# Moving the low half of the key rows from GpSimd to VectorE in the expert stage

## The chip, the cores and the metric

The kernel runs on one core of one Trainium2 chip. The metric is the device time of one execution in microseconds, the median of several. TensorE (PE), VectorE (DVE), ScalarE (ACT), GpSimd (POOL) and SyncE (SP) each work through an instruction list of their own in a fixed order and wait for each other by semaphores. Plain transfers are issued from SP's queue, gathers from POOL's queue; 16 DMA engines carry both.

## The reference

Two transformer blocks over 512 tokens of width 1024. Each ends with a mixture of 16,384 single-row experts, which is what the change touches. Cut to that part (the first block's; the second block's is the same function with other names):

```
q = (xb @ w_q).reshape(PEER_BLOCK, PEER_HEADS, 2, PEER_QDIM // 2)
s = jnp.einsum('thsd,hsnd->thsn', q, sub_keys).astype(jnp.float32)
sv, si = lax.top_k(s, PEER_TOPK)
...
e = jnp.take_along_axis(cidx, pos, axis=-1)
g = jax.nn.softmax(top, axis=-1)
act = jax.nn.gelu(jnp.einsum('thkd,td->thk', u_tab[e], xb), approximate=False)
w = (g * act).astype(xb.dtype)
return jnp.einsum('thk,thkd->td', w, v_tab[e])
```

Every token picks 8 x 16 = 128 experts. Each picked expert has a key row in `u_tab` and a value row in `v_tab`, both 1024 wide. The result is the sum of the value rows, weighted by gate times gelu(key row . token).

## The kernel before

The function `peer` (line 1071) runs once per block, so twice in the program. Its long stage is the loop over `e` in `range(128)` (line 1255): one step is one block of 128 experts. The 512 tokens are treated in two ways.

The first three tiles of 128 tokens (384 tokens) are done densely. `emit_A` makes the products of a block's 128 key rows with all 384 tokens: `a_dma` loads the block's transposed key rows `ur` (line 1094), `a_hi` rounds them to a high half `uh` on ACT (line 1099), `a_lo` makes the low half `ul = ur - uh` (line 1105), and `a_mm` multiplies: 24 matmuls (lines 1112, 1113, 1115), then a gelu into `ga`. Products run 28 blocks ahead (`NA = 28`), so that step `e` makes block `e + 28`, up to step 99. Then step `e` multiplies `ga` by the gates of block `e` (`gbuf`, loaded once for four blocks) to `w`, splits `w` into `wh` (ACT, line 1268) and `wl` (DVE, line 1269) and the value rows `vr` into `vh` (ACT) and `vl` (DVE, line 1263), and adds 18 matmuls into `y` (lines 1293 to 1295).

The last tile of 128 tokens is done by gathers. For each of 128 slots, `g_u` has POOL gather one key row per token into `urow` (line 1229), and DVE multiplies it with the tokens and sums (line 1230). `g_v` gathers the value rows into `vrow` (line 1241), and DVE adds them, weighted, into `acc` (line 1243). That makes 256 gathers in a stage, 128 rows of 4 KB each, into three buffers of `urow` and three of `vrow`. The first 32 or so are `urow` alone, then both kinds alternate, and the last are `vrow` alone. The rooms `ur`, `uh`, `ul`, `vr`, `vh`, `vl`, `w`, `wh` and `wl` have two buffers each.

What sets the order: a scheduler, which works out when each instruction could start, puts the instructions of every engine into a fixed list when the program is built. One engine is exempt in this loop. The block `with tc.manual_schedule(engines={mybir.EngineType.Pool})` (line 1270) leaves POOL's instructions in program order: in each step first what `emit_A` gives POOL, then as many gathers as `want` says (line 1273), some 2.7 per step, spread over steps 2 to 98. POOL waits at a gather until DVE has freed one of the three buffers.

After step 99 there are no more products ahead, and a step has only its 18 matmuls. In the first stage steps 100 to 119 have `vl` made by POOL (line 1263), and from step 100 a side job makes rows of the second block's modulation (lines 794 to 825); at step 120 the last tile's sum is finished.

Of the kernel before, what the change touches and what calls it, by code (L numbers as in the profile page):

```python
# [23 lines left out]
def build(tc, I, out, dbg=None, stop=None):  # L24
# [28 lines left out]
    def rsqrt(ssq, n, scale, nm, eps=EPS):  # L53
        """1 / sqrt(ssq * scale + eps) for a [128, n] tile."""
        p = ssq.shape[0]
        v = sm.tile([p, n], F32, name=nm + "v", tag=f"rv{n}", bufs=2 if n > 8 else 4)
        V.tensor_scalar(out=v, in0=ssq, scalar1=scale, scalar2=eps, op0=OP.mult, op1=OP.add)
        h = sm.tile([p, n], I32, name=nm + "h", tag=f"rh{n}", bufs=2 if n > 8 else 4)
        V.tensor_scalar(out=h, in0=v.bitcast(I32), scalar1=1, scalar2=None, op0=OP.logical_shift_right)
        y = sm.tile([p, n], F32, name=nm + "y", tag=f"ry{n}", bufs=2 if n > 8 else 4)  # L60
        V.tensor_scalar(out=y.bitcast(I32), in0=h, scalar1=-1.0, scalar2=1597463007.0, op0=OP.mult, op1=OP.add)
        t = sm.tile([p, n], F32, name=nm + "t", tag=f"rt{n}", bufs=2 if n > 8 else 4)
        if n == 1:
            V.tensor_scalar(out=v, in0=v, scalar1=-0.5, scalar2=None, op0=OP.mult)
            for _ in range(3):
                V.scalar_tensor_tensor(out=t, in0=y, scalar=y, in1=v, op0=OP.mult, op1=OP.mult)
                V.scalar_tensor_tensor(out=y, in0=t, scalar=1.5, in1=y, op0=OP.add, op1=OP.mult)
            return y
        for _ in range(3):
            V.tensor_tensor(out=t, in0=y, in1=y, op=OP.mult)  # L70
            V.scalar_tensor_tensor(out=t, in0=t, scalar=-0.5, in1=v, op0=OP.mult, op1=OP.mult)
            V.scalar_tensor_tensor(out=y, in0=t, scalar=1.5, in1=y, op0=OP.add, op1=OP.mult)
        return y
# [5 lines left out]
    def transpose_split(src, ncol, hi, lo, dst, psum=None):  # L79
        """src [128, ncol*128] -> hi/lo[:, k, dst] for each 128-column chunk k."""  # L80
        for k0 in range(0, ncol, 4):
            n = min(4, ncol - k0)
            pool, tag = psum or (pst, "tr")
            pt = pool.tile([128, 4, 128], F32, name="pt", tag=tag)
            for k in range(n):
                T.transpose(pt[:, k, :], src[:, (k0 + k) * 128:(k0 + k + 1) * 128], ident)
            split(dst_view(pt[:, 0:n, :], dst, src=True), dst_view(hi[:, k0:k0 + n, :], dst), dst_view(lo[:, k0:k0 + n, :], dst))
# [6 lines left out]
    def ssq_of(src, junk, nm):  # L94
        """sum of squares along the free axis on the scalar engine"""
        s = sm.tile([src.shape[0], 1], F32, name=nm, tag="ssq")
        A.activation(out=junk, in_=src, func=AF.Square, accum_out=s)
        return s
# [6 lines left out]
    def load_w(W, k, c0, cn, pool=None, e=V):  # L105
        """rows of chunk k of a weight matrix, as high and low halves"""
        raw = wst.tile([128, 512], F32, name="wr", tag="wraw", bufs=3)
        if pool:
            hi, lo = pool[:, 0], pool[:, 1]
        else:  # L110
            hi = wst.tile([128, 512], F32R, name="wh", tag="whi", bufs=WB)
            lo = wst.tile([128, 512], F32R, name="wl", tag="wlo", bufs=WB)
        S.dma_start(out=raw[:, 0:cn], in_=W[k * 128:(k + 1) * 128, c0:c0 + cn])
        split(raw[:, 0:cn], hi[:, 0:cn], lo[:, 0:cn], e)
        return hi[:, 0:cn], lo[:, 0:cn]
# [14 lines left out]
    def proj(hiT, loT, W, K, c0, cn, evac, tiles=range(NT), pool=None):  # L130
        """token-major product: for each token tile, psum[128, cn] = h @ W[:, c0:c0+cn]"""
# [16 lines left out]
    def keep_w(pool, W, K, c0, cn=512, last=0, e=V):  # L148
        """a block of weight columns on chip, for products of one token tile after the other"""
        room = [pool.tile([128, 2, 512], F32R, name=f"wk{i}") for i in range(K)]  # L150
        return [load_w(W, k, c0, cn, room[(k + K - last) % K], e) for k in range(K)]
# [10 lines left out]
    def proj_rows(hiT, loT, ws, evac, then):  # L162
        """all token tiles in turn; then(t) follows two tiles behind"""
# [7 lines left out]
    # token order of everything after the first mixing: row p of tile r is token 4 p + r  # L171
# [6 lines left out]
    # =====================================================================  # L178
    # block 1: norm, input projection
    # =====================================================================  # L180
# [43 lines left out]
    def head_proj(pool, hi, lo, W, c0, nh, hd, tiles, finish, first=None, wait=False):  # L224
        """nh heads of width hd divided by their root mean square; finish(t, heads, scale)"""
        n, nt = nh * hd, len(tiles)
        raw = first
# [90 lines left out]
    def cmul(o_r, o_i, a_r, a_i, b_r, b_i, pool, shape, conj_b=False, e=V):  # L318
        """o = a * b (or a * conj b)"""
# [22 lines left out]
    # powers a^0 .. a^8  # L342
# [14 lines left out]
    # c a^n: real part and negated imaginary part  # L357
# [16 lines left out]
    # unit phases e^{i Theta j}, Theta = 8 theta, and the decay of a chunk  # L374
# [37 lines left out]
    def coefficients():  # L412
        s5x = ExitStack()
        s5t = s5x.enter_context(tc.tile_pool(name="s5t", bufs=1, side="right"))
        # chunk-input coefficients, transposed to [(s, c), pair, (g2, p)]
# [12 lines left out]
        # block-Toeplitz matrices [(s, c_in), g, (t, c_out)], two groups of a pair at a time  # L428
# [94 lines left out]
    def norm_T(xt, gain, hi, lo, sl, pool, inplace=False, two=False):  # L523
        """rmsnorm of a [128, 1024] tile with gain, transposed and split"""
# [218 lines left out]
    def softmax_row(ps, n, z, pool, tag="pe"):  # L743
        """exp(scores - max) with its sum"""
# [43 lines left out]
    def modulation(rows, pool, psum, tags, ptag, on_pool):  # L788
        """rows of the modulation; yields after each block of 128 x 1024 weights"""
# [64 lines left out]
    def queries(qp, Wq, hi, lo):  # L854
        """loads, halves and products of the 128-column blocks of the query weights"""
# [31 lines left out]
    def peer_route(rw, query, keysT, crep, E, GT, ahead, also, first):  # L887
        """expert indices (as float) and gates, [128, tile, 128 slots]

        Step l of 16 is one half of one head's query; the candidates of a head are  # L890
        looked up in the steps of the next head, and products of the first expert
        blocks run between the steps' products."""
# [23 lines left out]
        def top16(src, work, vals, idx, tiles):  # L916
            """the 16 largest of src[:, t] with their places, in order"""
# [96 lines left out]
        def more(e):  # L1014
            """product e, then the halves of block e + 2, whose room it frees"""
# [41 lines left out]
    def peer_front(nm, Wq):  # L1057
        """room for the transposed input, and for its making"""
# [11 lines left out]
    def peer(keysT_d, U, UT, Vt, front, finish, nm, side=None, also=None, then=None):  # L1070
# [31 lines left out]
        def a_lo(e):  # L1102
            raw, uh = ua[e]
            ul = ub.tile([128, 8, 128], F32R, name="ul", tag="ul")
            G.tensor_tensor(out=ul, in0=raw, in1=uh.bitcast(F32), op=OP.subtract)  # L1105
# [14 lines left out]
        def emit_A(e):  # L1120
            a_dma(e)
            a_hi(e)
            a_lo(e)
            a_mm(e)
# [32 lines left out]
        # slot-major indices and gates of the dense tokens  # L1157
        # first index = 16 a + b; rows a, b, second index (bf16 holds them) and gate
# [96 lines left out]
        for e in range(128):  # L1255
# [14 lines left out]
            with tc.manual_schedule(engines={mybir.EngineType.Pool}):  # L1270
                if e + NA < 128:
                    emit_A(e + NA)
# [52 lines left out]
    def fin1(t, acc, pool, psum):  # L1325
        """sum, then the first normalization of the second block"""
# [30 lines left out]
    def first_rows():  # L1357
        """the second block's first projection, by token tiles"""
# [12 lines left out]
    # lambda of the differential attention, on every partition  # L1371
# [48 lines left out]
    # =====================================================================  # L1420
    # block 2
    # =====================================================================
# [23 lines left out]
    def rope_proj(which, dst, c0, nh, col, first=None):  # L1446
        """projection, head norm, rotation and transposition of nh heads, from 128-column chunk c0 of dst on"""
# [77 lines left out]
    # the residual waits in memory while its room holds the values  # L1525
# [52 lines left out]
    def projT(hi, lo, W, K, c0, evac, n=4):  # L1578
        """feature-major product: for each 128-column chunk, psum[128, tokens] = W[:, chunk].T @ h"""
# [190 lines left out]
def sincos(nc, pool, ang, shape, c, s):  # L1770
    """cosine and sine of any angle: reduced by whole turns in three exact steps"""
# [20 lines left out]
def host_arrays(a):  # L1792
    """layout only"""
# [73 lines left out]
```

## Time and profile before

| | |
|---|---|
| median of 3 runs | 4070.91 us (4067.79 to 4075.79) |
| profiled execution, first to last instruction | 4090.4 us |
| PE busy | 3876.8 us, 95% |
| DVE busy | 3004.6 us, 73% |
| POOL busy | 2145.8 us, 52% |
| ACT busy | 1654.8 us, 40% |
| moved by DMA | 784.31 MB, mean 192 GB/s |

The profiled execution has no time of its own beside its span, which is 19.5 us longer than the median of the runs. Times of the trace count from the span's start. The long stage of the first block runs from about 975 to 1940 us, that of the second from about 3115 to 4060 us. "Busy" adds up the time in which an engine works on an instruction; a share of the whole span says little, since the stages have different limits. "Idle before, releaser" names what ended an engine's wait.

### The profile page before, as it was taken

Reading aid. Unit: us, or ns where it says so; the run is one execution under the profiler, and the core shown is the slowest. Engines: PE = TensorE matmul, PEld = TensorE weight load, DVE = VectorE, ACT = ScalarE, POOL = GpSimd, SP = SyncE. Lnnn points to the kernel's source line nnn. Section 1 sums busy time; section 2 is a strip of 40 time slices with the busy share of each in tenths; the row PEclk is TensorE's granted clock in tenths of the full one; section 3 lists DMA queues with packets and bytes.
Section 4 is the critical chain, followed back from the end, with each engine's and each line's share of the span. In section 5 each row is a group of like instructions: output and inputs, shape, how many; then the busy total and the mean of one; then the engine's idle time right before and its main releaser. Section 6 shows DMA issues by size and latency. Waiting matters only on the chain. (4 is left out here: it accounts for less than half of the span.)

```text
span 4090.4 us, 53234 instructions
## 1 busy us (share of the span) xinstructions
PE 3876.8 (95%) x19062; PEld 3370.2 (82%) x19062; DVE 3004.6 (73%) x5440; ACT 1654.8 (40%) x2567; POOL 2145.8 (52%) x1353
## 2 busy tenths in 40 slices
PE   6999998899999999989899988999899999999999
PEld 5777788899899999877777766788899899989887
DVE  8456489884787778777756566689884788878765
ACT  3454432454333333323444567332454333333333
POOL 3000057655777777754424433257655777776740
PEclk8999999999999999999999989999999999999999
DMA  3333132236898889986222323332237898888874
GB/s 112 99 111 106 52 113 79 101 134 230 302 319 320 315 311 315 318 275 221 90 81 57 93 75 100 102 114 79 98 134 250 299 322 314 311 306 308 299 254 150
DMA packets 330057, 784.31 MB, mean 192 GB/s; under 512 B 32048, under 2 KB 148864, under 8 KB 326400
## 3 DMA queue, kind: packets, MB, share of 16 engines
q1 hardware_dynamic: 252608, 499.86, 36.4%
q0 software_dynamic: 77184, 281.05, 19.5%
q8 instruction: 150, 2.46, 0.2%
q14 instruction: 115, 0.94, 0.1%
HBM read 722.98 MB, written 56.65 MB: 191 GB/s over the span
## 5 line engine op out<-in xcount | busy, mean ns | idle before, releaser
L1105 POOL TENSOR_TENSOR ul<-ur,uh 128x1024 fp32r<-128x1024 f32 x256 | 676.5, 2643 | 378.0 <-ACT uh L1099 259.5
L1112 PE MATMUL pa<-phi,uh 128*128 128x384 f32 x2048 | 695.5, 340 | 0.8 <-ACT ga L1117 0.8
L1113 PE MATMUL pa<-plo,uh 128*128 128x384 f32 x2048 | 694.8, 339 | 0.0
L1294 PE MATMUL y<-vl,wh 128*128 128x512 f32 x1536 | 606.2, 395 | 26.1 <-DVE vl L1263 22.4
L1295 PE MATMUL y<-vh,wl 128*128 128x512 f32 x1536 | 609.2, 397 | 11.3 <-DVE wl L1269 11.3
L1293 PE MATMUL y<-vh,wh 128*128 128x512 f32 x1536 | 603.8, 394 | 1.3 <-ACT wh L1268 1.2
L1243 DVE SCALAR_TENSOR_TENSOR acc<-vrow,act,acc 128x1024 f32<-128x1024 f32 x256 | 392.3, 1532 | 196.6 <-DMA vrow<-in_expert_v_dram,ei 99.5
L1230 DVE SCALAR_TENSOR_TENSOR urow<-urow,hgat 128x1024 f32<-128x1024 f32 x256 | 392.0, 1534 | 172.0 <-DMA urow<-in_peer_u_dram,ei 85.5
L1268 ACT CAST wh<-w 128x384 fp32r<-128x384 f32 x256 | 131.2, 513 | 736.0 <-PE y L1294 483.8
L1099 ACT CAST uh<-ur 128x1024 fp32r<-128x1024 f32 x256 | 269.3, 1052 | 382.9 <-PE pa L1113 149.2
L1115 PE MATMUL pa<-phi,ul 128*128 128x384 f32 x2048 | 402.5, 339 | 18.0 <-POOL ul L1105 17.9
L1112 PEld LDWEIGHTS pa<-phi,uh 128*128 128x128 f32 x2048 | 389.0, 190 | 10.0 <-ACT ga L1117 1.1
L1113 PEld LDWEIGHTS pa<-plo,uh 128*128 128x128 f32 x2048 | 389.1, 190 | 9.6
L1263 DVE TENSOR_TENSOR vl<-vr,vh 128x1024 fp32r<-128x1024 f32 x236 | 353.4, 1498 | 34.6 <-DMA ur<-in_peer_uT_dram 16.2
L1115 PEld LDWEIGHTS pa<-phi,ul 128*128 128x128 f32 x2048 | 362.0, 190 | 19.9 <-POOL ul L1105 19.9
L1206 PE MATMUL pgg<-oh,oh 128*128 128x128 f32 x1536 | 374.3, 421 | 4.4 <-DVE oh L1198 3.9
L1206 PEld LDWEIGHTS pgg<-oh,oh 128*128 128x128 f32 x1536 | 369.9, 337 | 7.1 <-issue 5.3
L1294 PEld LDWEIGHTS y<-vl,wh 128*128 128x128 f32 x1536 | 290.5, 189 | 93.5 <-DVE vl L1263 32.3
L1295 PEld LDWEIGHTS y<-vh,wl 128*128 128x128 f32 x1536 | 290.5, 189 | 85.0 <-DVE wl L1269 22.5
L1293 PEld LDWEIGHTS y<-vh,wh 128*128 128x128 f32 x1536 | 290.8, 189 | 55.5 <-ACT wh L1268 1.7
L77 DVE TENSOR_TENSOR wl<-wr,wh 128x512 fp32r<-128x512 f32 (+1 forms) x276 | 198.9, 729 | 148.9 <-ACT wh L76 148.8
L1200 POOL TENSOR_TENSOR oh<-oha,ohb 128x1024 f32<-128x1024 f32 x72 | 218.2, 3033 | 143.9 <-PE pgg L1206 104.5
(539 smaller groups left out, 7694.7 us busy)
## 6 DMA issues: line engine op xcount, KB each, us to landing
vr<-in_peer_v_dram SPq DMA_DIRECT2D x128, 512.0 KB
ur<-in_peer_uT_dram SPq DMA_DIRECT2D x128, 512.0 KB
vr<-in_expert_v_dram SPq DMA_DIRECT2D x128, 512.0 KB
ur<-in_expert_uT_dram SPq DMA_DIRECT2D x128, 512.0 KB
gbuf<-Gd SPq DMA_DIRECT2D x64, 768.0 KB
Gd<-stg SPq DMA_DIRECT2D x24, 1920.0 KB
wr<-in_w_in_dram SPq DMA_DIRECT2D x104, 256.0 KB
war<-in_w_ada_dram SPq DMA_DIRECT2D x24, 512.0 KB
```

The source lines that it names most:

```text
L1099: A.copy(out=uh, in_=ua[e])
L1105: G.tensor_tensor(out=ul, in0=raw, in1=uh.bitcast(F32), op=OP.subtract)
L1112: T.matmul(pa, uh[:, k, :], hi[:, k, 0:NDT], start=(k == 0), stop=False)
L1113: T.matmul(pa, uh[:, k, :], lo[:, k, 0:NDT], start=False, stop=False)
L1115: T.matmul(pa, ul[:, k, :], hi[:, k, 0:NDT], start=False, stop=(k == 7))
L1206: T.matmul(pg[:, j, :], oh2[:, :, 4 * q + j], oh1[:, :, 4 * q + j], start=True, stop=True)
L1230: V.scalar_tensor_tensor(out=row, in0=row, scalar=1.0, in1=hg_, op0=OP.mult, op1=OP.mult, accum_out=act[:, k:k + 1])
L1243: V.scalar_tensor_tensor(out=acc, in0=vrow.pop(k - 2), scalar=act[:, k - 2:k - 1], in1=acc, op0=OP.mult, op1=OP.add)
L1263: (G if side and EV <= e < EW else V).tensor_tensor(out=vl, in0=vr, in1=vh.bitcast(F32), op=OP.subtract)
L1293: T.matmul(y[t][c], wh[:, ts], vh[:, cs_], start=(e_ == 0), stop=False)
L1294: T.matmul(y[t][c], wh[:, ts], vl[:, cs_], start=False, stop=False)
L1295: T.matmul(y[t][c], wl[:, ts], vh[:, cs_], start=False, stop=(e_ == 127))
```

## The change

`a_lo` and `emit_A` get a parameter for the engine. The call in the long loop passes VectorE; all other calls (routing, `run_ahead`) keep GpSimd. In each of the two stages 100 subtractions of 128x1024 (`ul`) go from POOL to DVE. In the loop POOL then has only the gathers left inside the block with the manual order (and `vl` of steps 100 to 119 in the first stage). Elsewhere the diff only removes comments and docstrings; the line numbers stay.

```
-        def a_lo(e):
+        def a_lo(e, eng=G):
             raw, uh = ua[e]
             ul = ub.tile([128, 8, 128], F32R, name="ul", tag="ul")
-            G.tensor_tensor(out=ul, in0=raw, in1=uh.bitcast(F32), op=OP.subtract)
+            eng.tensor_tensor(out=ul, in0=raw, in1=uh.bitcast(F32), op=OP.subtract)
             ua[e] = (uh, ul)
...
-        def emit_A(e):
+        def emit_A(e, eng=G):
             a_dma(e)
             a_hi(e)
-            a_lo(e)
+            a_lo(e, eng)
             a_mm(e)
...
             with tc.manual_schedule(engines={mybir.EngineType.Pool}):
                 if e + NA < 128:
-                    emit_A(e + NA)
+                    emit_A(e + NA, V)
                 want = min(len(ev), max(0, (len(ev) * (e + 1 - GS) + GE - 1) // GE))
```

The scheduler's lists change with it. PE's list is the same instruction for instruction. On POOL, at the start of the first block's long stage, the list before was this (`ul` is the low half, `urow` and `vrow` the gathers of key and value rows):

```order
L1224 MEMSET acc 128x1024
L794 MEMSET ones 128x1
L1105 TENSOR_TENSOR ul<-ur,uh 128x1024 x2
L1229 DMA urow<-in_peer_u_dram,ei 128x1024 x3
L1105 TENSOR_TENSOR ul<-ur,uh 128x1024
L1229 DMA urow<-in_peer_u_dram,ei 128x1024 x3
```

At the same place POOL's list now is:

```order
L1224 MEMSET acc 128x1024
L1229 DMA urow<-in_peer_u_dram,ei 128x1024 x3
L1241 DMA vrow<-in_peer_v_dram,ei 128x1024
L1229 DMA urow<-in_peer_u_dram,ei 128x1024
L794 MEMSET ones 128x1
L1229 DMA urow<-in_peer_u_dram,ei 128x1024 x30
L1241 DMA vrow<-in_peer_v_dram,ei 128x1024
```

Before, a `ul`, which needs the key rows of its step, stood between every two or three gathers. Now one gather follows the other, and nothing on POOL but a free buffer holds the next one back.

On DVE, in the middle of the same stage, the list before ran like this; one `w` (line 1267) is one step:

```order
L1263 TENSOR_TENSOR vl<-vr,vh 128x1024
L1269 TENSOR_TENSOR wl<-w,wh 128x384
L1230 SCALAR_TENSOR_TENSOR urow,act<-urow,hgat 128x1024
L1267 TENSOR_TENSOR w<-gbuf,ga 128x384
L1243 SCALAR_TENSOR_TENSOR acc<-vrow,act,acc 128x1024
L1263 TENSOR_TENSOR vl<-vr,vh 128x1024
L1269 TENSOR_TENSOR wl<-w,wh 128x384
L1230 SCALAR_TENSOR_TENSOR urow,act<-urow,hgat 128x1024
L1267 TENSOR_TENSOR w<-gbuf,ga 128x384
```

DVE's list at the corresponding place now is:

```order
L1230 SCALAR_TENSOR_TENSOR urow,act<-urow,hgat 128x1024
L1243 SCALAR_TENSOR_TENSOR acc<-vrow,act,acc 128x1024 x2
L1269 TENSOR_TENSOR wl<-w,wh 128x384
L1263 TENSOR_TENSOR vl<-vr,vh 128x1024
L1267 TENSOR_TENSOR w<-gbuf,ga 128x384
L1230 SCALAR_TENSOR_TENSOR urow,act<-urow,hgat 128x1024
L1105 TENSOR_TENSOR ul<-ur,uh 128x1024
L1230 SCALAR_TENSOR_TENSOR urow,act<-urow,hgat 128x1024
L1243 SCALAR_TENSOR_TENSOR acc<-vrow,act,acc 128x1024 x2
L1269 TENSOR_TENSOR wl<-w,wh 128x384
```

A step has one `ul` more, and the gathered rows' work is moved forward. Counted over DVE's list between the `w` rows, steps 16 to 55 have 10.4 of the lines 1230 and 1243 per four steps before and 17.0 now. Step 4 to 11 now have 30 of line 1230 and 3 of line 1243; steps 12 to 55 have 188 of both; steps 56 to 63 have 29 of line 1243; the list has none after that. Before, the last of them stood at steps 100 to 103. The second stage reads the same within one or two.

## Rows read from the trace of the kernel before

**Rows 1.** Windows of both long stages; the first line names the columns.

```profile
core 0: us, PE busy (x) PEld busy (x) DVE busy (x) ACT busy (x) POOL busy (x), PEclk, DMA share, GB/s
1100.00:1700.00 600.00, 600.00 (x3043) 546.44 (x3042) 491.35 (x509) 216.38 (x295) 447.62 (x261) 1.00 0.90 318
980.00:1511.00 531.00, 525.75 (x2649) 475.36 (x2648) 419.32 (x456) 190.53 (x261) 392.51 (x228) 1.00 0.88 312
3122.00:3653.00 531.00, 524.09 (x2632) 473.08 (x2631) 418.75 (x451) 187.41 (x257) 385.40 (x226) 1.00 0.87 309
```

**Rows 2.** Groups by line, PE, 1100 to 1700: count, busy, mean ns, idle before.

```profile
L1293 PE MATMUL y<-vh,wh 128*128 128x512 f32 x432 | 168.1, 389 | 0.0
```

**Rows 3.** Groups by line, DVE, 1100 to 1700.

```profile
L1230 DVE SCALAR_TENSOR_TENSOR urow<-urow,hgat 128x1024 f32<-128x1024 f32 x95 | 152.6, 1607 | 48.7 <-DMA urow<-in_peer_u_dram,ei 48.2
L1243 DVE SCALAR_TENSOR_TENSOR acc<-vrow,act,acc 128x1024 f32<-128x1024 f32 x95 | 150.5, 1584 | 62.3 <-DMA vrow<-in_peer_v_dram,ei 62.1
L1263 DVE TENSOR_TENSOR vl<-vr,vh 128x1024 fp32r<-128x1024 f32 x73 | 110.9, 1520 | 0.0
```

**Rows 4.** Groups by line, POOL, 1100 to 1700.

```profile
L1105 POOL TENSOR_TENSOR ul<-ur,uh 128x1024 fp32r<-128x1024 f32 x73 | 192.8, 2641 | 105.6 <-ACT uh L1099 100.8 <-PE pa L1115 2.5 <-issue 1.7
```

**Rows 5.** Timeline of DVE, 990 to 1014: start, duration, what, idle before.

```profile
992.12 1.23 DVE L1230 SCALAR_TENSOR_TENSOR urow<-urow,hgat 128x1024 f32<-128x1024 f32 x1 [1.99 <-DMA urow<-in_peer_u_dram,ei]
...
1005.62 1.21 DVE L1263 TENSOR_TENSOR vl<-vr,vh 128x1024 fp32r<-128x1024 f32 x1
1006.76 0.55 DVE L1269 TENSOR_TENSOR wl<-w,wh 128x384 fp32r<-128x384 f32 x1
1007.22 1.21 DVE L1230 SCALAR_TENSOR_TENSOR urow<-urow,hgat 128x1024 f32<-128x1024 f32 x1
...
1008.37 1.21 DVE L1230 SCALAR_TENSOR_TENSOR urow<-urow,hgat 128x1024 f32<-128x1024 f32 x1
...
1013.14 1.23 DVE L1230 SCALAR_TENSOR_TENSOR urow<-urow,hgat 128x1024 f32<-128x1024 f32 x1 [3.08 <-DMA urow<-in_peer_u_dram,ei]
```

**Rows 6.** Timeline of DVE, 1739 to 1790.

```profile
1739.09 1.28 DVE L1243 SCALAR_TENSOR_TENSOR acc<-vrow,act,acc 128x1024 f32<-128x1024 f32 x1
1740.29 1.22 DVE L1263 TENSOR_TENSOR vl<-vr,vh 128x1024 fp32r<-128x1024 f32 x1
...
1787.74 1.28 DVE L1243 SCALAR_TENSOR_TENSOR acc<-vrow,act,acc 128x1024 f32<-128x1024 f32 x1 [4.25 <-DMA vrow<-in_peer_v_dram,ei]
```

**Rows 7.** Timeline of POOL, 985 to 1014.

```profile
985.94 1.69 POOL L1229 DMA_INDIRECT urow<-in_peer_u_dram,ei  x1 [2.51 <-DVE urow L1230]
...
1005.97 1.69 POOL L1229 DMA_INDIRECT urow<-in_peer_u_dram,ei  x1 [1.37 <-DVE urow L1230]
1008.71 1.68 POOL L1229 DMA_INDIRECT urow<-in_peer_u_dram,ei  x1 [1.05 <-DVE urow L1230]
1010.41 2.42 POOL L1105 TENSOR_TENSOR ul<-ur,uh 128x1024 fp32r<-128x1024 f32 x1
```

**Rows 8.** The page's DMA issues: queue, count, KB each.

```profile
vr<-in_peer_v_dram SPq DMA_DIRECT2D x128, 512.0 KB
ur<-in_peer_uT_dram SPq DMA_DIRECT2D x128, 512.0 KB
...
gbuf<-Gd SPq DMA_DIRECT2D x64, 768.0 KB
```

**Rows 9.** Windows with much DMA, columns as in rows 1.

```profile
3700.00:3720.00 20.00, 20.00 (x102) 18.04 (x101) 14.12 (x16) 7.10 (x10) 14.42 (x9) 1.00 0.99 350
...
1696.00:1704.00 8.00, 8.00 (x42) 7.30 (x41) 6.80 (x7) 4.45 (x7) 4.80 (x3) 1.00 1.02 395
```

**Rows 10.** What PE waited for, 1700 to 1940: us, times, longest.

```profile
PE y L1295 <- DVE wl L1269: 9.2, 4, 5.7
PE y L1294 <- DVE vl L1263: 3.9, 4, 1.2
```

**Rows 11.** What PE waited for, 3690 to 3980.

```profile
PE y L1294 <- DVE vl L1263: 7.3, 6, 2.9
```

More of the change, by code (lines that the diff above doesn't have):

```diff
@@ L1100, in a_hi, with a_lo @@
             ua[e] = (ua[e], uh)
-        def a_lo(e):
+        def a_lo(e, eng=G):
             raw, uh = ua[e]
             ul = ub.tile([128, 8, 128], F32R, name="ul", tag="ul")
-            G.tensor_tensor(out=ul, in0=raw, in1=uh.bitcast(F32), op=OP.subtract)
+            eng.tensor_tensor(out=ul, in0=raw, in1=uh.bitcast(F32), op=OP.subtract)
             ua[e] = (uh, ul)
@@ L1118, in a_mm, with emit_A @@
             gas[e] = ga
-        def emit_A(e):
+        def emit_A(e, eng=G):
             a_dma(e)
             a_hi(e)
-            a_lo(e)
+            a_lo(e, eng)
             a_mm(e)
@@ L1271, in peer @@
                 if e + NA < 128:
-                    emit_A(e + NA)
+                    emit_A(e + NA, V)
                 want = min(len(ev), max(0, (len(ev) * (e + 1 - GS) + GE - 1) // GE))
```

## The prediction

> **What bounds the kernel now.** I read the windows of the two long stages first, since a share of the whole span mixes stages. The reader is to see that in the middle of the stage PE is busy for all 600 of 600 us at full granted clock, while DVE has 491 and POOL 448, and that the DMA engines are at 0.90 of their time with 318 GB/s [rows 1]. So PE sets the pace: 432 matmuls of one kind, six per step, are 72 steps in 600 us, 8.3 us each [rows 2]. POOL has slack and its `ul` mostly waits for ACT (100.8 of 105.6 us idle, [rows 4]); nothing is to be won in that part by a faster POOL. Next I read the groups by line of DVE: its gathered rows cost a mean of 1607 and 1584 ns, though one alone takes 1.21 to 1.28 us [rows 3, 5, 6], and it stood idle 111 us for gathers that had not landed [rows 3]. Then the timelines of DVE and POOL for what one gather costs in time, the DMA issues for bytes, and last PE's own waits near the end of each stage [rows 5 to 11].
>
> **What the change removes.** 100 `ul` per stage leave POOL, 2.64 us each [rows 4]. On POOL itself that is worth nothing while PE is the bound. It has two other effects.
>
> First, DVE is no longer stretched. POOL's gathers do not stretch it: the `urow` at 1008.37 took 1.21 us although a gather was being issued from 1008.71 on [rows 5, 7]. The long means of rows 3 go with the `ul` on POOL, and with them gone I take the undisturbed spacing of starts: `vl` 1.14 (1005.62 to 1006.76), `wl` 0.46, `urow` 1.15 [rows 5], `acc` 1.20 [rows 6]; `ul` has the shape of `vl`, and `w` that of `wl`. The Trainium skill, "SBUF — State Buffer", section on the port pair that DVE and GpSimd share, says that a DVE instruction with two inputs in SBUF blocks only against a GpSimd instruction that reads SBUF; the stretched rows before agree. Without that rule, at the means of rows 3 for all 1024-wide work, a middle step would need 2 x 1.52 + 0.92 + 4.27 x 1.595 = 10.8 us of DVE and my sum would be some 71 us higher, 4331.
>
> Second, nothing paces the gathers any more. Before, the `ul` of a step stood between them on POOL; now only a free buffer holds them back, and DVE's new list, which is fixed, takes 17.0 gathered rows per four steps where it took 10.4 (counted with the change). All 256 gathers of a stage fall into its first 64 steps instead of its first 104. PE's list is unchanged, so these 64 steps cost at least 64 x 8.3 = 531 us, and what comes on top is lost: steps 64 to 99 stay bound by PE at 8.3 us and give nothing back.
>
> **What it adds, step by step, for one stage.**
>
> DVE, middle steps (12 to 55, 188 gathers, 4.27 per step): 4.27 x 1.175 + 2 x 1.14 (`ul`, `vl`) + 2 x 0.46 (`w`, `wl`) = 8.22 us, against PE's 8.3. It fits by 0.1 us and has no room for any wait. Behind a gather that DVE waits for stand `vl`, `wl` and `ul` of the step, which PE needs.
>
> DMA, middle steps: a gather is 128 rows of 4 KB, 0.524 MB, as `ur` and `vr` are, and `gbuf` is 0.786 MB per four steps [rows 8]. So 188 x 0.524 + 44 x (1.049 + 0.197) = 153.4 MB. PE's pace would need 153.4 MB in 365.2 us, 420 GB/s. The trace has 350 GB/s in the fullest 20 us and 395 in the fullest 8 us [rows 9]; the mean in the stage is 318 [rows 1]. Nothing sustains 420. I take 350, the longer of the two windows: 438.3 us, 9.96 per step, **+73.1 us**. At 395 it is 388.4 us, +23.2. If instead DVE's waits per gathered row stay what they are (111 us over 190 rows is 0.58, [rows 3]), a step is 8.22 + 4.27 x 0.58 = 10.7 us, 471.7 in all, +106.5.
>
> The head, steps 4 to 11, 30 `urow` (the 3 `acc` go in beside): one kind alone has three buffers. A buffer's turn is its DVE work 1.15, until POOL's next issue 0.35 (1005.62 to 1005.97), and 7.17 from that issue until DVE can start (1005.97 to 1013.14) [rows 5, 7]: 8.67 us for three, 2.89 each. 30 x 2.89 = 86.7 us against 8 x 8.3 = 66.4: **+20.3 us**. With the shorter landing of 6.18 (985.94 to 992.12) it is 2.56 each, +10.4. With the pace that `acc` alone shows, 14 intervals in 48.65 us, 3.47 each [rows 6], it is +37.7.
>
> The tail of the gathers, steps 56 to 63, 29 `acc`, by the same three prices: 83.8 - 66.4 = **+17.4 us**, ends +7.8 and +34.2.
>
> Sum of a stage +110.8, two stages +221.6. Some of this PE already loses: of the first 531 us of each stage it is idle 5.2 and 6.9 us [rows 1], which I subtract: -12.2.
>
> **What comes back.** With the gathers over at step 64, the last 64 steps have DVE and DMA to spare. PE's waits for DVE near the end, 9.2 + 3.9 us in the first stage and 7.3 in the second [rows 10, 11], stand where the gathers' last work and the side job compete with `vl` and `wl`. I credit all: -20.4. What else is moved costs nothing: the side job's loads and its POOL work go from step 100 forward to about step 62, into steps with 1.2 MB of traffic in 8.3 us (150 GB/s) and an empty POOL.
>
> Against the profiled execution: 4090.4 + 221.6 - 12.2 - 20.4 = 4279. The median of the runs lies 19.5 us below that span, so the same +189 on 4070.9 gives **4260 us**.
>
> **The rivals.**
>
> *DMA has more to give.* The windows at 395 GB/s [rows 9] came without a backlog; with six gathers queued it may hold that, and landings take 6.18 us. Then a stage loses 10.4 + 23.2 + 7.8 = 41.4, and 2 x 41.4 - 32.6 = +50: 4121. Against it: the 20 us window with 0.99 of the DMA engines' time has 350.
>
> *DVE's order stalls it at every gather.* DVE has no slack left, waits in order, and each wait then falls on PE. Its price is the upper ends above: 2 x (37.7 + 106.5 + 34.2) - 32.6 = +324: 4395. For it: 111 us of waits now, at only 2.6 gathers per step. Against it: more gathers in flight and no `ul` in their way on POOL.
>
> *Not slower.* The place is the same middle of the stage. If DMA carries 420 GB/s there, and gathers land so early that DVE's 8.22 us are hardly interrupted, PE keeps its 8.3 us through the first 64 steps and only the credits remain: -12.2 - 20.4 = -33, 4038. It decides from 420 GB/s on, with a buffer's turn under 6.6 us (8 steps of 8.3 us for 30 rows, 2.2 each). The Trainium skill, "HBM Reference", Specifications, speaks for it: a core that streams alone measures about 425 GB/s, by which the middle would take 361 us, no more than PE. No stretch of this trace sustains that, and the shortest turn I see is 7.68 us, so I give it little.
>
> **How the numbers follow.** Forecast (DMA near 350 GB/s, turns near 8.7 us) 0.60, its own range 4180 to 4330; more DMA 0.17; stalls at every gather 0.16; not slower 0.07. The range 4120 to 4395 leaves out the last and what lies beyond the middle of the stalls. Within 0.2% is within 8 us, which is what a measurement can tell; only the edge between the last case and the first rival falls there, 0.02. Faster 0.06, slower 0.92.
>
> **What would show it.** In the new profile: PE idle in the first two thirds of both long stages, with DVE `vl`, `wl` or `ul` as releaser and DVE in turn waiting for `urow` and `vrow`; DMA near 350 GB/s in the middle, then near 150; no `urow` or `vrow` after about two thirds of the stage; means of lines 1230, 1243 and 1263 near 1.2 to 1.3 us; steps of about 10 us there and of 8.3 afterwards. I am wrong if PE stays busy throughout, if the gathers still reach the stage's end, or if DMA passes 390 GB/s for hundreds of us.

## The result, and the profile after

| | median us | range of 5 runs | profiled span | mean granted clock |
|---|---|---|---|---|
| before, same chip | 4075.79 | 4067.79 to 4083.75 | 4090.4 | 0.975 |
| after | 4367.67 | 4358.82 to 4383.76 | 4382.0 | 0.955 |

The changed kernel takes 1.0707 times as long (95% interval 1.0685 to 1.073), 292 us more. The sign and the range of the forecast hold; the time lies above the range of the likeliest case (4180 to 4330) and nearer to the rival of stalls at every gather (4395).

I first looked for the place. The value products (line 1295) of the first long stage start from 972.8 to 2105.7 us, before from 971.2 to 1960.1; those of the second from 3264.9 to 4372.8, before from 3117.0 to 4081.1. The stages are 144.0 and 143.8 us longer, 287.8 of the 292 us.

The page's totals of the changed kernel, span and busy time by engine:

```profile
span 4382.0 us, 53215 instructions
PE 3965.8 (91%) x19062; PEld 3423.4 (78%) x19062; DVE 2956.0 (67%) x5640; ACT 1649.7 (38%) x2567; POOL 1565.6 (36%) x1153
```

POOL lost 580 us of work, and DVE, with 200 instructions more, is busy for 49 us less than before. PE does the same work and is busy for 89 us more: some of it ran slower. Windows of the changed kernel, with the columns of [rows 1]: the first 531 us of the first stage, the middles of both stages, and the time after the gathers.

```profile
980.00:1511.00 531.00, 443.68 (x2030) 386.00 (x2029) 397.97 (x518) 143.94 (x202) 259.67 (x204) 0.93 0.88 312
1080.00:1570.00 490.00, 402.20 (x1837) 349.66 (x1835) 363.45 (x456) 130.33 (x183) 235.14 (x184) 0.93 0.89 315
3370.00:3850.00 480.00, 400.25 (x1821) 347.77 (x1820) 364.28 (x457) 127.70 (x180) 228.55 (x184) 0.92 0.89 314
1700.00:1950.00 250.00, 248.04 (x1257) 225.61 (x1256) 118.76 (x143) 90.69 (x122) 0.00 (x0) 1.00 0.53 171
```

No engine is full in the middle: PE has 402 of 490 us, DVE 363, POOL 235, and DMA stands at 0.89 with 315 GB/s, no more than the 318 of [rows 1]. A stage in which nothing is full is bound by a wait. The groups by line of DVE from 1100 to 1600 answer to [rows 3]:

```profile
L1243 DVE SCALAR_TENSOR_TENSOR acc<-vrow,act,acc 128x1024 f32<-128x1024 f32 x103 | 132.0, 1281 | 14.1 <-DMA vrow<-in_peer_v_dram,ei 13.6
L1230 DVE SCALAR_TENSOR_TENSOR urow<-urow,hgat 128x1024 f32<-128x1024 f32 x87 | 106.4, 1223 | 114.3 <-DMA urow<-in_peer_u_dram,ei 114.2
L1105 DVE TENSOR_TENSOR ul<-ur,uh 128x1024 fp32r<-128x1024 f32 x45 | 55.0, 1222 | 0.0
L1263 DVE TENSOR_TENSOR vl<-vr,vh 128x1024 fp32r<-128x1024 f32 x44 | 53.8, 1223 | 0.0
```

and those of POOL, where `ul` no longer stands as in [rows 4]:

```profile
L1241 POOL DMA_INDIRECT vrow<-in_peer_v_dram,ei x103 | 138.9, 1348 | 237.8 <-DVE acc L1243 212.0 <-issue 8.8 <-DVE act L1234 6.1
L1229 POOL DMA_INDIRECT urow<-in_peer_u_dram,ei x85 | 101.6, 1195 | 26.3 <-issue 25.7 <-DMA vrow<-in_peer_v_dram,ei 0.6
```

DVE is unstretched, as forecast. But it waits almost only for key rows (114.2 us against 13.6 for value rows), and POOL, which issues both, waits almost only at value rows (212.0 us, for `acc` to free a buffer), hardly ever at key rows. The two waits belong together, as one place shows. Timeline of POOL in the changed kernel:

```profile
1302.89 0.94 POOL L1229 DMA_INDIRECT urow<-in_peer_u_dram,ei  x1 [0.30 <-DMA vrow<-in_peer_v_dram,ei]
1311.85 1.01 POOL L1241 DMA_INDIRECT vrow<-in_peer_v_dram,ei  x1 [8.03 <-DVE acc L1243]
1313.17 1.47 POOL L1229 DMA_INDIRECT urow<-in_peer_u_dram,ei  x1 [0.30 <-issue]
```

and of DVE at the same time:

```profile
1305.51 1.22 DVE L1105 TENSOR_TENSOR ul<-ur,uh 128x1024 fp32r<-128x1024 f32 x1
...
1309.15 1.23 DVE L1230 SCALAR_TENSOR_TENSOR urow<-urow,hgat 128x1024 f32<-128x1024 f32 x1 [2.33 <-DMA urow<-in_peer_u_dram,ei]
...
1310.30 1.28 DVE L1243 SCALAR_TENSOR_TENSOR acc<-vrow,act,acc 128x1024 f32<-128x1024 f32 x1
...
1319.93 1.23 DVE L1230 SCALAR_TENSOR_TENSOR urow<-urow,hgat 128x1024 f32<-128x1024 f32 x1 [2.16 <-DMA urow<-in_peer_u_dram,ei]
```

A `urow` buffer is free at 1305.51. Its next gather stands on POOL's queue behind a `vrow` gather, which waits 8.03 us for the `acc` of 1310.30; so it is issued at 1313.17, 7.7 us after its buffer was free, and DVE can use the row at 1319.93. DVE's wait then holds up `vl`, `wl` and `ul` behind it, and PE with them. Sums of the waits from 980 to 1640:

```profile
POOL vrow L1241 <- DVE acc L1243: 234.9, 76, 9.3
DVE urow L1230 <- DMA urow<-in_peer_u_dram,ei: 142.9, 73, 6.6
...
PE y L1294 <- DVE vl L1263: 113.4, 40, 6.0
```

PE's clock falls as well. Two neighbouring windows, columns as above:

```profile
1308.00:1316.00 8.00, 2.92 (x13) 2.41 (x13) 6.30 (x9) 3.42 (x6) 2.48 (x2) 0.89 0.54 186
1316.00:1324.00 8.00, 8.00 (x29) 6.69 (x28) 5.81 (x7) 1.47 (x2) 3.98 (x3) 0.68 0.91 320
```

In the first window PE is idle for 5 us. In the next it is busy for all 8 us, but at a mean granted clock of 0.68, between its levels of 1.2 and 2.4 GHz. Its timeline shows both levels: the matmuls into `y` start 0.43 us apart at first, and 0.23 us apart from 1321.14 on.

```profile
1316.05 0.63 PE L1293 MATMUL y<-vh,wh 128*128 128x512 f32 x1
1316.48 0.63 PE L1294 MATMUL y<-vl,wh 128*128 128x512 f32 x1
...
1321.14 0.40 PE L1293 MATMUL y<-vh,wh 128*128 128x512 f32 x1
1321.37 0.39 PE L1294 MATMUL y<-vl,wh 128*128 128x512 f32 x1
```

The Trainium skill, "TensorE: Matmul & The Clock Gate", section on HAM oscillation, describes this: after waits between bursts the next burst starts throttled. These rows agree.

### The profile page after: what moved, and what is told of

Same layout as the page of the kernel before. It is cut to its first block, busy times and chain, and to the rows that moved or that the text cites. A ratio compares the mean times of both kernels' runs of the same rounds, so it can differ in the third digit from the quotient of the medians.

```text
span 4382.0 us, 53215 instructions
## 1 busy us (share of the span) xinstructions
PE 3965.8 (91%) x19062; PEld 3423.4 (78%) x19062; DVE 2956.0 (67%) x5640; ACT 1649.7 (38%) x2567; POOL 1565.6 (36%) x1153
## 5 line engine op out<-in xcount | busy, mean ns | idle before, releaser
L1294 PE MATMUL y<-vl,wh 128*128 128x512 f32 x1536 | 648.7, 422 | 233.5 <-DVE vl L1263 230.2
L1295 PE MATMUL y<-vh,wl 128*128 128x512 f32 x1536 | 638.0, 415 | 5.5 <-DVE wl L1269 5.5
L1293 PE MATMUL y<-vh,wh 128*128 128x512 f32 x1536 | 633.5, 413 | 2.3 <-ACT wh L1268 1.2
L1294 PEld LDWEIGHTS y<-vl,wh 128*128 128x128 f32 x1536 | 310.9, 202 | 331.0 <-DVE vl L1263 263.1
L1230 DVE SCALAR_TENSOR_TENSOR urow<-urow,hgat 128x1024 f32<-128x1024 f32 x256 | 313.1, 1223 | 287.7 <-DMA urow<-in_peer_u_dram,ei 147.3
L1115 PE MATMUL pa<-phi,ul 128*128 128x384 f32 x2048 | 403.8, 340 | 17.5 <-POOL ul L1105 17.4
L1243 DVE SCALAR_TENSOR_TENSOR acc<-vrow,act,acc 128x1024 f32<-128x1024 f32 x256 | 328.1, 1282 | 65.6 <-DMA vrow<-in_peer_v_dram,ei 33.9
L1295 PEld LDWEIGHTS y<-vh,wl 128*128 128x128 f32 x1536 | 311.5, 203 | 76.3 <-DVE wl L1269 9.7
L1269 DVE TENSOR_TENSOR wl<-w,wh 128x384 fp32r<-128x384 f32 x256 | 151.3, 592 | 317.1 <-ACT wh L1268 317.1
L1105 DVE TENSOR_TENSOR ul<-ur,uh 128x1024 fp32r<-128x1024 f32 x200 | 244.6, 1223 | 131.8 <-ACT uh L1099 100.6
L1262 ACT CAST vh<-vr 128x1024 fp32r<-128x1024 f32 x256 | 268.0, 1048 | 72.8 <-DMA vr<-in_peer_v_dram 35.6
```

The costliest lines, as they stand in the source:

```text
L1105: eng.tensor_tensor(out=ul, in0=raw, in1=uh.bitcast(F32), op=OP.subtract)
L1115: T.matmul(pa, ul[:, k, :], hi[:, k, 0:NDT], start=False, stop=(k == 7))
L1230: V.scalar_tensor_tensor(out=row, in0=row, scalar=1.0, in1=hg_, op0=OP.mult, op1=OP.mult, accum_out=act[:, k:k + 1])
L1243: V.scalar_tensor_tensor(out=acc, in0=vrow.pop(k - 2), scalar=act[:, k - 2:k - 1], in1=acc, op0=OP.mult, op1=OP.add)
L1262: A.copy(out=vh, in_=vr)
L1293: T.matmul(y[t][c], wh[:, ts], vh[:, cs_], start=(e_ == 0), stop=False)
```

## The experiments

Two things could be at fault: that the gathers crowd into the first half of the stage (nothing paces them), or how they get through POOL's queue and the DMA engines once crowded. All ratios are to the kernel before, run on the same chip (4083.6 to 4084.4 us). The changed kernel was timed where the kernel before took 4075.8, so differences from it in us hold to within about 8. The letters in the expectations are the theories as they stood then.

**Pacing put back (e1_pace).** An eighth of each `ul` stays on POOL, so that the scheduler again lays the gathers out beside it: 159 by step 64, as before.

```
-            eng.tensor_tensor(out=ul, in0=raw, in1=uh.bitcast(F32), op=OP.subtract)
+            if eng is G:
+                G.tensor_tensor(out=ul, in0=raw, in1=uh.bitcast(F32), op=OP.subtract)
+            else:
+                G.tensor_tensor(out=ul[:, 7:8], in0=raw[:, 7:8], in1=uh[:, 7:8].bitcast(F32), op=OP.subtract)
+                V.tensor_tensor(out=ul[:, 0:7], in0=raw[:, 0:7], in1=uh[:, 0:7].bitcast(F32), op=OP.subtract)
```

> The changed kernel, with POOL keeping one eighth of each ul of the long loop (columns 896 to 1023) and DVE the other seven eighths. DVE's list then takes the gathered rows at the pace of before (159 of 256 by step 64), while DVE still makes nearly all of ul. Theory A (the lost pace: gathers crowd into the first 64 steps): a middle step needs 2.62 x 1.175 + 3.2 = 6.3 us of DVE, PE sets the pace again, 4040 to 4080 us. Theory B (the load: 100 more instructions per stage on DVE, in order, are the cost): above 4200 us, since seven eighths of that load are still there.

4058.69 us, ratio 0.9942 (0.992 to 0.9964), as theory A said. The whole loss is gone, with seven eighths of the move kept. From 1100 to 1700 PE is nearly full again:

```profile
1100.00:1700.00 600.00, 595.72 (x3006) 541.18 (x3005) 458.38 (x573) 214.47 (x293) 289.45 (x258) 1.00 0.90 313
```

**Crowding alone (e2_early).** The kernel before, `ul` on POOL, with the due time of the gathers moved: `GE = 99` becomes `GE = 63`, 247 gathers by step 64.

> The kernel before, ul still on POOL, but with the gathers spread over steps 2 to 62 instead of 2 to 98 (247 of 256 by step 64). Theory A (crowding is the cost, whoever makes ul): slower than before by 150 to 350 us, 4220 to 4420. Theory B (DVE's 100 more subtractions are the cost): within 20 us of before, 4055 to 4095.

4294.09 us, ratio 1.0516 (1.0487 to 1.0546). Theory A again: crowding costs 210 us without the move. But the limit is another one than in the changed kernel. Here DVE is nearly full, stretched by the `ul` on POOL (its gathered rows have means of 1503 and 1560 ns), and DMA carries more:

```profile
1080.00:1510.00 430.00, 386.58 (x1827) 334.00 (x1828) 402.51 (x409) 129.61 (x180) 359.56 (x227) 0.97 0.96 349
```

**Pacing by program order (e6_man).** The changed kernel with DVE, too, left in program order: 157 gathers by step 64.

```
-            with tc.manual_schedule(engines={mybir.EngineType.Pool}):
+            with tc.manual_schedule(engines={mybir.EngineType.Pool, mybir.EngineType.DVE}):
```

> The changed kernel, with DVE exempt from the scheduler's order inside the block that already exempts POOL: ul and the gathered rows stand on DVE in program order, 157 of 256 by step 64, and POOL has the gathers alone. Theory A (lost pace): 4040 to 4080 us, because the fixed list of DVE paces the gathers. Theory B (load on DVE): above 4200 us. If POOL's empty queue is what lets transfers crowd whatever DVE's list says, also above 4200 us.

4130.43 us, ratio 1.0131 (1.0103 to 1.0159). Paced and still slower than before: crowding is not the only cause, and theory A's 4040 to 4080 is missed. Waits, 980 to 1640:

```profile
POOL vrow L1241 <- DVE acc L1243: 330.5, 76, 13.5
...
DVE urow L1230 <- DMA urow<-in_peer_u_dram,ei: 176.4, 44, 7.5
```

Again POOL stands at `vrow` and DVE waits for `urow`, with DMA at 0.82 from 1100 to 1700. So the second theory: the queue. A `vrow` gather waiting for its buffer blocks the `urow` gather behind it.

**A fourth buffer (e8_vbuf4).** The changed kernel, one more `vrow` buffer in the first stage. The second stage has no room for it, and is the control. (Tiles of the side job that use the same buffers get the fourth too; those lines are not shown.)

```
-                vrow[k] = gw.tile([128, 1024], F32, name="vrow", tag="vrow")
+                vrow[k] = gw.tile([128, 1024], F32, name="vrow", tag="vrow", bufs=4 if nm == "1" else 3)
...
```

> The changed kernel with four instead of three buffers for vrow in the first stage alone (the second stage has no room and serves as a comparison). In the changed kernel POOL stood 240 us of the first stage at a vrow gather that waited for a free buffer, with the next urow gather queued behind it, and DVE stood 143 us for urow. Theory Q (POOL's queue: the urow gather is issued late because it stands behind the blocked vrow gather): the first stage gets shorter by 40 to 100 us and DVE's wait for urow falls below 80 us; total 4270 to 4330. Theory D (bandwidth of DMA sets the step of 11.2 us): the first stage stays within 15 us, total 4350 to 4385.

4293.52 us, ratio 1.0519 (1.049 to 1.0547). The first stage takes 1048.3 us instead of 1132.9; the second 1111.3, as in the changed kernel (1107.9). First the middle of the first stage, then of the second:

```profile
1080.00:1510.00 430.00, 388.43 (x1870) 342.89 (x1869) 369.89 (x468) 130.09 (x183) 248.48 (x190) 0.97 0.99 366
3290.00:3800.00 510.00, 424.28 (x1919) 368.36 (x1918) 383.15 (x479) 133.87 (x189) 248.74 (x196) 0.91 0.90 314
```

With POOL let through, DMA rises from 314 to 366 GB/s at 0.99 of its engines' time: only now is it the bound (e4 below tests this). The waits of the first stage:

```profile
POOL vrow L1241 <- DVE acc L1243: 144.0, 78, 6.4
...
DVE urow L1230 <- DMA urow<-in_peer_u_dram,ei: 76.8, 56, 4.3
```

The starts and ends in the two traces show the queue itself. In steps 12 to 55 of the first stage of the changed kernel a `urow` buffer stands free for a mean of 6.2 us before its next gather is issued, a `vrow` buffer for 0.75 us. In e8 it is 3.3 and 0.6 us. (In the kernel before it is 8.5 us, behind `ul`, and costs nothing there, since a step takes 2.6 gathered rows and not 4.3.) But a fourth buffer also puts more bytes in flight, so a theory of latency alone would say the same.

**The buffer freed sooner (e10_lag1).** The changed kernel, three buffers; `acc` follows one gather behind instead of two.

```
-            if k >= 2:
-                V.scalar_tensor_tensor(out=acc, in0=vrow.pop(k - 2), scalar=act[:, k - 2:k - 1], in1=acc, op0=OP.mult, op1=OP.add)
+            if k >= 1:
+                V.scalar_tensor_tensor(out=acc, in0=vrow.pop(k - 1), scalar=act[:, k - 1:k], in1=acc, op0=OP.mult, op1=OP.add)
...
-        for k in range(128 + 34):
+        for k in range(128 + 33):
```

> The changed kernel, where acc of a value row stands one gather behind its issue instead of two (same three buffers, same bytes, gathers still crowded: 256 by step 64). The vrow gather on POOL then waits for an acc that DVE does one place earlier. Theory Q (the urow gather stands on POOL behind a vrow gather that waits for its buffer): both stages get what the fourth buffer gave the first stage, 60 to 100 us each, 4180 to 4260 us in all, with middle steps of 9.5 to 10 us and DMA near 366 GB/s. Theory R (the fourth buffer helped because more bytes were in flight, not because of the queue): 4340 to 4385.

4241.9 us, ratio 1.0389 (1.0354 to 1.0425): 126 us less than the changed kernel, both stages alike (1055.6 and 1048.5), without a buffer more; a free `urow` buffer waits 3.2 us for its gather. Theory R (4340 to 4385) is out. Waits of the first stage, then a window of its middle:

```profile
POOL vrow L1241 <- DVE acc L1243: 158.4, 87, 4.8
...
DVE urow L1230 <- DMA urow<-in_peer_u_dram,ei: 71.3, 62, 4.1
```

```profile
1100.00:1500.00 400.00, 359.84 (x1733) 316.68 (x1732) 346.66 (x436) 122.31 (x172) 225.20 (x175) 0.97 0.99 367
```

**Both (e11_manlag1).** The edits of e6 and e10 together.

> The kernel with DVE's program order (gathers paced, 158 of 256 by step 64) and acc one gather behind instead of two. With two behind it took 4130 us, and POOL stood 434 us of the first stage at vrow. Theory Q: with the queue's wait eased nothing is left of the cost, 4050 to 4090 us. If pacing by DVE's list is itself what stalls DVE at each gather, it stays at 4115 to 4145.

4028.41 us, ratio 0.9868 (0.9834 to 0.9901): 56 us faster than the kernel before, and 22 us below the least that theory Q had given. None is clearly faster. PE is full and at full clock:

```profile
980.00:1511.00 531.00, 530.90 (x2688) 482.76 (x2687) 414.52 (x528) 195.79 (x267) 229.80 (x168) 1.00 0.91 320
```

```profile
POOL vrow L1241 <- DVE acc L1243: 233.1, 66, 10.4
...
DVE urow L1230 <- DMA urow<-in_peer_u_dram,ei: 25.3, 18, 4.4
```

POOL's wait is as long as in the changed kernel (234.9) and harmless: here it waits because the rows are there ahead of their use. DVE waits 25.3 us for key rows against 142.9, and PE no longer waits for `vl` at all, against 113.4 us.

**Does the lag matter to e1 (e12_pacelag1)?** e1's edit and e10's.

> The version with one eighth of ul on POOL (4059 us, faster than before by 0.6%) with acc one gather behind instead of two. If POOL's queue still costs it something, DVE's 203 us of waiting for gathers in the first stage fall and the time goes to 4030 to 4055; if PE is already the bound there, 4050 to 4070, no change that can be told.

4056.73 us, ratio 0.9924 (0.9896 to 0.9952), not to be told from e1's 4058.69. Where a piece of `ul` spaces the gathers on POOL's queue, freeing `vrow` sooner wins nothing. The trace of e1 shows why: POOL waits at its piece of `ul`, and hardly at all at a `vrow` (980 to 1640; e1's lines are shifted by up to 4).

```profile
POOL ul L1108 <- ACT uh L1099: 145.0, 36, 10.0
POOL ul L1108 <- PE pa L1119: 123.4, 35, 6.0
...
POOL vrow L1245 <- DVE acc L1247: 0.3, 1, 0.3
```

The waits of five kernels in that window, us, show which of them counts:

| | POOL at `vrow` for `acc` | DVE for `urow` and `vrow` | PE for `vl` | time |
|---|---|---|---|---|
| before | none | 137.9 | 5.2 | 4075.8 |
| after | 234.9 | 171.0 | 113.4 | 4367.7 |
| e1 | 0.3 | 166.0 | 9.4 | 4058.7 |
| e6 | 330.5 | 176.4 | 30.9 | 4130.4 |
| e11 | 233.1 | 25.3 | none | 4028.4 |

Neither POOL's wait nor DVE's tells the slow kernels (e6, after) from the others. PE's does, and PE is the engine that bounds the stage. With the gathers spread out (before, e1) DVE can wait long for rows without PE noticing.

**Half the bytes (e4_half4).** e8, with every gather fetching half a row (`U2` is the table seen as half rows, `ei2` twice the index) and DVE reading that half twice. The value rows are gathered in the same way.

```
-            G.indirect_dma_start(out=row, out_offset=None, in_=U, in_offset=bass.IndirectOffsetOnAxis(ap=ei[:, TL, k:k + 1], axis=0))
+            G.indirect_dma_start(out=row[:, 512:1024], out_offset=None, in_=U2, in_offset=bass.IndirectOffsetOnAxis(ap=ei2[:, k:k + 1], axis=0))
```

> The changed kernel with four vrow buffers in the first stage, and gathers that fetch only half of each row (256 KB instead of 512 KB a gather; DVE's work is the same length, reading the fetched half twice; so the last token tile is computed from half rows). It asks whether DMA is the next bound once POOL's queue is eased. First stage, four buffers: its middle steps took 9.70 us at 366 GB/s and 0.99 of the DMA engines. Theory DMA-next: with half the bytes they come to 8.3 to 8.6 us. Theory DVE-next (8.22 us of work in order, any wait shows): they stay above 9.3. Second stage, three buffers: if the step of 11.1 us is mostly landing time in the queue's cycle, it falls to 9 to 10 us; total 4130 to 4220.

4189.26 us, ratio 1.0259 (1.0224 to 1.0294). The two stages part. With four buffers a middle step falls from 9.70 to 8.74 us (384.7 for 44 steps), just above the range for DMA as the bound. With three it falls from 11.11 only to 10.29 us, above the 9 to 10 expected, though DMA is idle more than a quarter of the time. A row there can be used sooner (6.0 us after its issue on average, against 8.1), but a free `urow` buffer still waits 7.2 us for its gather. Middles of the first and the second stage:

```profile
1080.00:1450.00 370.00, 360.68 (x1796) 324.75 (x1795) 354.80 (x450) 126.11 (x177) 248.67 (x182) 0.99 0.83 275
3230.00:3670.00 440.00, 387.14 (x1816) 339.62 (x1815) 358.46 (x450) 128.63 (x180) 231.58 (x184) 0.94 0.72 231
```

So in the changed kernel itself the DMA engines' rate is not what binds.

**The edits on the kernel before.** e13_beforelag1 is the kernel before with e10's edit; e15_beforemanlag1 has e6's as well, `ul` staying on POOL.

> The kernel before, ul on POOL, with acc one gather behind instead of two and nothing else. It asks what of the 4028 us (ul on DVE, DVE in program order, acc one behind) is the last of these alone. If POOL's queue was already eased by the ul between the gathers, 4060 to 4090, no change that can be told; if the lag was costing the kernel before as well, 4030 to 4055.

> The kernel before, ul on POOL, with DVE in program order and acc one gather behind: the version of 4028 us without the move of ul. Theory M (the move itself is worth something once the gathers are paced: no ul on POOL, so DVE is not stretched and a gather is issued at once): 4055 to 4090, with mean times of urow and acc near 1.5 us again. Theory N (the order alone did it): 4020 to 4040.

4078.46 us, ratio 0.9978 (0.9959 to 0.9997), and 4083.79 us, ratio 0.9998 (0.9977 to 1.0019): next to nothing. So e11's gain needs the move; between e15 and e11, which differ in it alone, it is worth 55 us. Whether this comes from a DVE that is not stretched or from gathers that no `ul` holds up was not tried apart; the rows show both. Key rows on DVE from 1100 to 1700, e15:

```profile
L1230 DVE SCALAR_TENSOR_TENSOR urow<-urow,hgat 128x1024 f32<-128x1024 f32 x94 | 139.6, 1485 | 114.0 <-DMA urow<-in_peer_u_dram,ei 113.9
```

and e11:

```profile
L1230 DVE SCALAR_TENSOR_TENSOR urow<-urow,hgat 128x1024 f32<-128x1024 f32 x92 | 112.1, 1219 | 6.0 <-DMA urow<-in_peer_u_dram,ei 6.0
```

**And `vl` of steps 100 to 119 (e14_vlv).** e11 with `EV = 120`: these go to DVE too.

> The version of 4028 us with vl of steps 100 to 119 of the first stage on DVE instead of POOL, so that POOL has no arithmetic in the loop at all. DVE gets 20 x 1.2 us more in steps of 4.1 us of PE, where it is busy about 0.8 of the time with the side job; PE waited only some 8 us in the first stage. 4020 to 4040, no change that can be told; above 4045 if DVE becomes the bound there.

4032.5 us, ratio 0.9851 (0.9822 to 0.988): no change from e11.

The four kernels with `ul` on DVE, us:

| | `acc` two behind | one behind |
|---|---|---|
| DVE's list by the scheduler (gathers crowded) | 4367.7 (after) | 4241.9 (e10) |
| DVE in program order (paced) | 4130.4 (e6) | 4028.4 (e11) |

Freeing the buffer sooner is worth 126 or 102 us, the order 237 or 214. Program order changes more than the pace; e1 and e2 move the pace by other means and point the same way.

## Why the prediction was right in sign and short in size

The bounds of the steps are the starts of `w` on DVE; those of steps 12 and 56 in the changed kernel, first stage:

```profile
1076.98 0.55 DVE L1267 TENSOR_TENSOR w<-gbuf,ga 128x384 f32<-128x384 f32 x1
...
1573.25 0.55 DVE L1267 TENSOR_TENSOR w<-gbuf,ga 128x384 f32<-128x384 f32 x1
```

Likewise steps 4 and 64 at 987.45 and 1662.82, and in the second stage 3282.97, 3368.66, 3857.69 and 3943.34. What each stretch costs over PE's 8.3 us a step:

| term, us | forecast per stage | first stage | second stage |
|---|---|---|---|
| head, steps 4 to 11 | +20.3 | +23.1 | +19.3 |
| middle, steps 12 to 55 | +73.1 | **+131.1** | **+123.8** |
| tail, steps 56 to 63 | +17.4 | +23.2 | +19.3 |
| already lost before, steps 4 to 63 | -12.2 for both | -3.9 | -9.8 |
| comes back after step 64 | -20.4 for both | -25.0 | -11.1 |

The measured terms add up to 290 of the 292 us; those of the forecast to 189.

- *Not shown:* that POOL's relief is worth nothing in itself while PE is the bound. No run has it alone; e15 to e11 shows that the move gains 55 us once gathers are paced and let through.
- *Right:* DVE is no longer stretched (1223, 1281, 1222 and 1223 ns). The Trainium skill, "SBUF — State Buffer", section "Who interferes with whom", says that only a GpSimd instruction that reads SBUF blocks a two-input DVE instruction; with POOL left to issue gathers, no stretch is left in these means.
- *Right:* all gathers fall into the first 64 steps (the last are issued at 1647.73 and 3930.18, before the `w` of step 64), and e1 and e2 show that this crowding decides the sign.
- *Right:* head and tail, by the turn of three buffers. A turn was priced at 8.67 us; the traces have a mean of 9.0 and 8.5 us in the heads of the two stages, 8.7 and 8.6 in the tails.
- *Wrong:* the middle's +73.1. The step that failed is "I take 350" GB/s as what a middle step waits for. The changed kernel moved 315 there. The wait was in POOL's order: two kinds of gather on one queue, of which the one with a free buffer stands behind the one without. With that eased (e8, e10) the first stage's middle takes 9.70 us a step in e8 at 366 GB/s; the forecast had 9.96 at 350. So the sum was right for a kernel whose POOL queue was let through. I had priced POOL's gathers by turns of three buffers of one kind alone and never asked what the other kind does to it: in the middle of the first stage a `urow` turn takes 15.6 us, 6.2 of them with the buffer free and its gather not yet issued. The upper bound, +106.5, was too low for the same reason: it kept the waits of a POOL that `ul` paced. That the time still lies inside the range, near the rival's 4395, is partly luck: the rival has the middle too small by 17 to 25 us a stage and head and tail together too large by 26 to 33.
- *Not in the sum:* the clock. In the 490 us window there are 43.4 steps at 11.28 us; at 8.3 they need 360 us of PE, but PE was busy for 402. So of the +131 some 88 us are idle time and up to 42 us slower work; an estimate from these rows. The granted clock of 0.93 over the 490 us, taken as time at half speed, accounts for at most 34.
- *Returns:* 36 us instead of 20.4. From step 64 on, PE's waits for DVE's `wl` and `vl` fall from 9.2 + 5.1 to 1.1 + 2.3 us in the first stage and from 7.3 us to none in the second, some 18 us in all, near the credit. Not in the credit: the granted clock in steps 100 to 126 of the first stage rises from 0.94 to 0.99.

"DMA has more to give" was half right: 366 to 367 GB/s is more than 350, but POOL's queue kept it from being asked. "Not slower" needed 420. The Trainium skill, "HBM Reference", Specifications, has about 425 GB/s for a core that streams alone; the fullest 300 us found in these traces have 372 (e10, 1080 to 1380), and e10's whole window above has 367 at 0.99 of the DMA engines' time.

Open: how the 237 us of order divide into pace and the rest of the list. And no run issued key and value gathers so that neither can stand before the other; that one holds up the other is shown by the traces and by what e8 and e10 did to it.

## What to carry to other kernels

An instruction on an in-order queue can be what paces the transfers behind it; before moving it, count what will be issued earlier and how deep the buffers let it run. Where two kinds of gather share a queue, the one whose buffer is freed late delays the other: free that buffer sooner. Judge by the wait of the engine that bounds the stage: the queue's wait for buffers is as long in the best kernel as in the slowest, and DVE's wait for rows is long in kernels that lose nothing by it. Fix the order first, then try the move again: the same edit cost 292 us here and, between two kernels that had both other edits (e15 and e11), gained 55.

## What the hardware showed that I had not expected

A mix of gathers and plain loads held 366 and 367 GB/s for 430 and 400 us at 0.99 of the DMA engines' time. And a short idle time of PE can cost twice: after 5 us without work the next 8 us ran at a mean of 0.68 of the clock, with matmuls 0.43 instead of 0.23 us apart.
